# One decoder layer on one core: where the second half of the tokens gets the low parts of its weights

## The chip, the core and the metric

The kernel runs on one core of a Trainium2 chip. The metric is the device time of one launch, in microseconds (us). Three runs of the kernel before took 3326.43, 3331.45 and 3336.54 us; the median is 3331.45 us. One further run was recorded by the hardware profiler: it took 3347.84 us, of which 3346.1 us are the span of the recorded instructions. A matter of 0.3% (10 us) is about what a comparison of two versions can tell from no change.

The engines of the core are called PE (matrix products), DVE (vector work), ACT (activation functions and copies), POOL (here it issues the gathers) and SP (here it issues all other DMA transfers). Each engine works through its own instructions in a fixed order and waits on semaphores for the others.

## What is computed

One layer over 1024 tokens of width 1024, all in fp32:

```python
z = x @ w_in                       # 9 column groups, width 7184
ua = causal_depthwise_conv(lru_x)  # branch A: RG-LRU, 8 channel blocks, a scan over time
ya = rg_lru(ua) * gelu(lru_y)
yb = rmsnorm(gla_chunked(q, k, v, log_f)) * silu(gla_r)   # branch B: 4 heads
m = sigmoid(gate_a) * ya + sigmoid(gate_b) * yb
x = layer_norm(ALPHA * x + m @ w_out)
ple = sigmoid(x @ ple_gate_w) * (p @ ple_proj_w)
# PEER: 8 heads, 16 of 16384 one-neuron experts each
hid = gelu(einsum("td,ted->te", x, u_tab[idx]))
ffn = einsum("te,ted->td", gate * hid, v_tab[idx])
out = layer_norm(ALPHA * x + ffn + ple)
```

## The kernel before

The tokens are worked in two halves of 512 (`HT`). For each half, `mixer` projects the tokens, runs the two branches and merges them, and `post` does the output product, the first layer norm, the scores of the experts, and the gate of the per-layer input. Then come the experts. Four of the eight blocks of 128 tokens (`GT`) gather their experts' rows one by one: for each of 128 selections POOL gathers a u row for every token (`ug`, line 837), DVE multiplies and sums it (line 839), later POOL gathers v rows (`vg`, line 866) and PE adds them up, four gathers in eight products at a time (`ffn`, line 873). The gathered tiles take turns in seven buffers (`ROWS`), so a gather waits until DVE or PE is done with an older one. The other four blocks (`DT`) are worked in `dense`: all 16384 experts for 512 tokens, with a dense table of gates (`dense_gates`, line 978).

The gathers begin at the end of the first half and go on to the end of the program. A generator hands out their steps while the second half's mixer, its `post` and then `dense` are recorded; a scheduler then sets each engine's order by its own estimate of when things are ready. So changing one thing can shift every engine's order from there on.

An fp32 product is made of three products of a faster type: each operand is split into a high part (a rounded copy, made by ACT) and a low part (the rest, source minus high part, made by DVE), and `mm3` (lines 251 to 254) multiplies high by high, high by low and low by high. Weights come in pieces of 128 rows by 1024 columns of fp32 (512 KB). `weights` loads a piece (`raw`, line 261) and makes the high part `wh_...` and the low part `wl_...`, each with two buffers in turn. Both halves of the tokens use the same weights. In the first half the low part is split off by DVE (line 249) and, for the first `LOW` pieces, also written to DRAM (line 275); in the second half, where a stored low part exists, it is read back instead (line 266) and only ACT's copy (line 267) is made:

```python
        key = (src.tensor.name, src.offset)
        if low.get(key) is not None:
            nc.sync.dma_start(l.bitcast(F32), low[key])
            nc.scalar.activation(h, raw, AF.Copy)
        else:
            split(h, l, raw)
            if key not in low:
                n = len(low)
                low[key] = None
                if n < LOW:
                    low[key] = dram.tile(shape, F32, name=f"low{n}")
                    nc.sync.dma_start(low[key], l.bitcast(F32))
```

With `LOW = 60` these are the 56 pieces of a mixer (`zx`, `zy`, `ga`, `gr`, `gb`, `zv` eight each, `zq` and `zk` four each) and the first 4 of the 8 pieces of the output product (`mix`).

Of the kernel before, what the change touches and what calls it, by code (L numbers as in the profile page):

```python
# [50 lines left out]
ROWS = 7  # L51
RING = 10

LOW = 60

TG = 8

# [7 lines left out]
def kernel(ctx: ExitStack, tc: tile.TileContext, a: dict, out: bass.AP, tap=None):  # L65
# [190 lines left out]
    def weights(src, name, shape):  # L256
# [11 lines left out]
# [7 lines that stand above are left out]
# [898 lines left out]
```

## Time and profile before

| stretch of the span (us) | what runs | PE busy | DVE busy | PE clock | DMA share |
|---|---|---|---|---|---|
| 15 to 415 (400) | mixer, first half | 390.11 | 250.05 | 0.98 | 0.44 |
| 647 to 1120 (473) | mixer, second half, with gathers | 423.26 | 378.14 | 0.92 | 0.77 |
| 1120 to 1650 (530) | post, second half, gate table, gathers | 401.75 | 464.00 | 0.89 | 0.85 |
| 1650 to 3290 (1640) | dense experts, gathers | 1608.49 | 1010.23 | 0.99 | 0.92 |
| whole span 3346.1; profiled run 3347.84 | | 3034.9 | 2303.3 | 0.95 | |
| median of three runs 3331.45 | | | | | |

[...] DMA share is how busy the 16 DMA engines were. A stretch is read by asking which engine is nearly always busy in it, and, where none is, what the engines wait for.

### The profile page before, as it was taken

What the parts mean: (1) busy time and instruction counts of PE and PEld (TensorE: products, weight loads), DVE (VectorE), ACT (ScalarE), POOL (GpSimd) and SP (SyncE); (2) the same over time, 40 slices, a digit from 0 to 9 for tenths busy, and PEclk for the clock granted to TensorE, in tenths of its full rate; (3) what the DMA queues carried; (4) which work ended last, traced back from release to release, by engine and by line L of the source; (5) the groups of instructions that cost most, each with busy time, mean ns of one, the idle gap of its engine ahead of it and who ended that gap; (6) DMA issues with size and microseconds to landing.
All of it is one profiled execution on the core that took longest, in us unless ns stands there. A gap on an engine that the chain in (4) does not pass through costs nothing.

```text
span 3346.1 us, 48006 instructions
## 1 busy us (share of the span) xinstructions
PE 3034.9 (91%) x17160; PEld 2318.8 (69%) x17160; DVE 2303.3 (69%) x5663; ACT 1233.1 (37%) x2130; POOL 1175.8 (35%) x1034
## 2 busy tenths in 40 slices
PE   8999988797999879658599999999999999999995
PEld 6788777576777666448467777777777777776662
DVE  7556558987788899888887766666666666564333
ACT  6443323253244565558433332222232222232220
POOL 0000000533421445440344544454444444453442
PEclk9999989897999899889799999999999999999997
DMA  5444444787877899976889999999989999999886
GB/s 172 146 164 152 143 159 131 296 289 251 315 242 253 319 305 327 300 256 171 309 316 353 330 333 334 342 329 335 336 321 347 347 336 338 343 327 321 315 288 241
DMA packets 364302, 939.73 MB, mean 281 GB/s; under 512 B 33920, under 2 KB 115968, under 8 KB 359968
## 3 DMA queue, kind: packets, MB, share of 16 engines
q0 software_dynamic: 147456, 536.94, 44.9%
q1 hardware_dynamic: 216608, 399.74, 34.4%
q8 instruction: 134, 2.20, 0.3%
q14 instruction: 104, 0.85, 0.1%
HBM read 854.76 MB, written 81.79 MB: 280 GB/s over the span
## 4 chain that ended last, share of the span: by engine, by line
PE 70%; DVE 11%; DMA 9%; ACT 4%; issue 4%; POOL 1%; another core or an unknown queue 0%; SPq 0%; POOLq 0%; DVEq 0%; ACTq 0%
PE ph L252 7%; PE ph L253 7%; PE ph L254 7%; PE ffn L873 7%; PE pv L253 7%; PE pv L252 7%; PE pv L254 7%; DMA vg<-in_peer_v_dram,idxT 3%; DMA ug<-in_peer_u_dram,idx 3%; DVE ug L839 2%; PE pg L978 1%; PE pgr L252 1%; PE pgr L254 1%; PE pgr L253 1%; PE pri L340 1%
## 5 line engine op out<-in xcount | busy, mean ns | idle before, releaser
L837 POOL DMA_INDIRECT ug<-in_peer_u_dram,idx x512 | 594.3, 1161 | 1319.7 <-DVE bs L766 615.4
L866 POOL DMA_INDIRECT vg<-in_peer_v_dram,idxT x512 | 580.1, 1133 | 819.2 <-DVE ug L839 402.3
L839 DVE SCALAR_TENSOR_TENSOR ug<-ug,x1g 128x1024 f32<-128x1024 f32 x512 | 621.3, 1220 | 298.6 <-DMA ug<-in_peer_u_dram,idx 242.3
L252 PE MATMUL ph<-x1h,uh 128*128 128x512 f32 x1024 | 408.5, 399 | 13.7 <-ACT uh L248 13.7
L253 PE MATMUL ph<-x1l,uh 128*128 128x512 f32 x1024 | 407.4, 398 | 0.0
L254 PE MATMUL ph<-x1h,ul 128*128 128x512 f32 x1024 | 406.4, 397 | 0.0
L253 PE MATMUL pv<-vl,wdh 128*128 128x512 f32 x1024 | 404.3, 395 | 0.3 <-DVE vl L249 0.3
L254 PE MATMUL pv<-vh,wdl 128*128 128x512 f32 x1024 | 400.4, 391 | 0.0
L252 PE MATMUL pv<-vh,wdh 128*128 128x512 f32 x1024 | 375.4, 393 | 24.0 <-ACT wdh L248 24.0
L248 ACT ACTIVATE vh<-vr 128x512 fp32r<-128x512 f32 x256 | 160.9, 631 | 567.8 <-PE pv L254 284.4
L873 PE MATMUL ffn<-vg,w 128*32 128x512 f32 x2048 | 264.5, 637 | 81.3 <-DMA vg<-in_peer_v_dram,idxT 80.4
L249 DVE TENSOR_TENSOR vl<-vr,vh 128x512 fp32r<-128x512 f32 x256 | 174.9, 688 | 207.0 <-ACT vh L248 177.6
L248 ACT ACTIVATE uh<-ur 128x512 fp32r<-128x512 f32 x256 | 160.3, 628 | 328.7 <-PE ph L253 233.2
L252 PEld LDWEIGHTS pv<-vh,wdh 128*128 128x128 f32 x1024 | 192.5, 188 | 76.7 <-ACT wdh L248 25.7
L252 PEld LDWEIGHTS ph<-x1h,uh 128*128 128x128 f32 x1024 | 192.4, 188 | 76.7 <-ACT uh L248 16.5
L249 DVE TENSOR_TENSOR ul<-ur,uh 128x512 fp32r<-128x512 f32 x256 | 175.1, 686 | 95.0 <-ACT uh L248 70.6
L253 PEld LDWEIGHTS pv<-vl,wdh 128*128 128x128 f32 x1024 | 192.8, 188 | 66.8 <-issue 16.8
L253 PEld LDWEIGHTS ph<-x1l,uh 128*128 128x128 f32 x1024 | 192.6, 188 | 57.3 <-issue 13.4
L254 PEld LDWEIGHTS ph<-x1h,ul 128*128 128x128 f32 x1024 | 192.4, 188 | 55.6 <-issue 8.4
L254 PEld LDWEIGHTS pv<-vh,wdl 128*128 128x128 f32 x1024 | 192.1, 188 | 46.5 <-issue 6.7
L873 PEld LDWEIGHTS ffn<-vg,w 128*32 128x32 f32 x2048 | 55.5, 113 | 215.9 <-issue 121.8
L978 PE MATMUL pg<-oi,oj 128*128 128x128 f32 x1024 | 165.4, 302 | 33.1 <-ACT oi L977 16.7
(475 smaller groups left out, 6056.2 us busy)
## 6 DMA issues: line engine op xcount, KB each, us to landing
ur<-in_uT_dram SPq DMA_DIRECT2D x256, 256.0 KB
vr<-in_peer_v_dram SPq DMA_DIRECT2D x256, 256.0 KB
g_d<-gst SPq DMA_DIRECT2D x32, 1024.0 KB
gt<-g_d SPq DMA_DIRECT2D x32, 1024.0 KB
raw_zx<-in_w_z_dram SPq DMA_DIRECT2D x16, 512.0 KB
raw_zv<-in_w_v_dram SPq DMA_DIRECT2D x16, 512.0 KB
raw_zy<-in_w_z_dram SPq DMA_DIRECT2D x16, 512.0 KB
raw_ga<-in_w_z_dram SPq DMA_DIRECT2D x16, 512.0 KB
```

What stands on the lines that cost most here:

```text
L248: nc.scalar.activation(h, src, AF.Copy)
L249: nc.vector.tensor_tensor(l, src, h, op=ALU.subtract)
L252: nc.tensor.matmul(o, wh, xh, start=first, stop=False)
L253: nc.tensor.matmul(o, wh, xl, start=False, stop=False)
L254: nc.tensor.matmul(o, wl, xh, start=False, stop=last)
L340: nc.tensor.matmul(o, wri[:, i, j], ua[:, i], start=True, stop=True)
L837: nc.gpsimd.indirect_dma_start(out=ug, out_offset=None, in_=a["peer_u"], in_offset=bass.IndirectOffsetOnAxis(ap=idx[:, s:s + 1], axis=0))
L839: nc.vector.scalar_tensor_tensor(ug, ug, 1.0, x1, op0=ALU.mult, op1=ALU.mult, accum_out=hid[:, s:s + 1])
L866: nc.gpsimd.indirect_dma_start(out=vg, out_offset=None, in_=a["peer_v"], in_offset=bass.IndirectOffsetOnAxis(ap=idxT[:, t:t + 1], axis=0))
L873: mm = nc.tensor.matmul(ffn[32 * c:32 * c + 32, e * 512:(e + 1) * 512], w32[:, c, r], rows_v[c][:, e * 512:(e + 1) * 512], start=ph == 0 a ...
L978: nc.tensor.matmul(o[:, r], oj[:, t], oi, start=True, stop=True)
```

## The change

```diff
-LOW = 60
+LOW = 0
```

With `LOW = 0` no low part is stored, so none is read back: the 60 stores of line 275 in the first half and the 60 read-backs of line 266 in the second are gone (31.5 MB each way), and the second half splits its 60 pieces itself: ACT's copy is made at line 248 instead of 267, the same copy, and DVE makes 60 more subtractions (line 249). A `raw` buffer, which ACT's copy alone used to free, is now freed by DVE's subtraction. Since the scheduler works from the new program, the second half is ordered anew on PE, DVE, ACT and SP. POOL's order is the same. At three places:

On DVE, in the second half's mixer at the end of the second head (`oT` and `m` are the head's output, `v`, `i` and `sc` belong to the routing of tokens to experts, `ug` to the gathers). Before:

```order
L474 SCALAR_TENSOR_TENSOR oT<-oT,gla_norm_g,pb 128x512 x2
L452 SCALAR_TENSOR_TENSOR tr<-tr,pgr 128x512
L480 TENSOR_TENSOR oT<-oT,tr 128x512
L839 SCALAR_TENSOR_TENSOR ug,hid<-ug,x1g 128x1024 x2
L484 SCALAR_TENSOR_TENSOR oT<-tb,oT 128x512
L485 TENSOR_TENSOR m<-m,oT 128x512
L725 MAX v_8057<-sc 128x8
L726 MAX_INDEX i_8058<-v_8057,sc 128x8
L727 MATCH_REPLACE sc<-v_8057,sc 128x128
L728 MAX v_8057<-sc 128x8
```

Now:

```order
L474 SCALAR_TENSOR_TENSOR oT<-oT,gla_norm_g,pb 128x512 x2
L249 TENSOR_TENSOR wl_gr<-raw_gr,wh_gr 128x1024
L725 MAX v_7937<-sc 128x8
L452 SCALAR_TENSOR_TENSOR tr<-tr,pgr 128x512
L726 MAX_INDEX i_7938<-v_7937,sc 128x8
L480 TENSOR_TENSOR oT<-oT,tr 128x512
L727 MATCH_REPLACE sc<-v_7937,sc 128x128
L728 MAX v_7937<-sc 128x8
L729 MAX_INDEX i_7938<-v_7937,sc 128x8
L839 SCALAR_TENSOR_TENSOR ug,hid<-ug,x1g 128x1024
L725 MAX v_7937<-sc 128x8
L249 TENSOR_TENSOR wl_gb<-raw_gb,wh_gb 128x1024
```

What moved: the low parts of the next weights (`gr`, `gb`) stand in DVE's row between the work of the head, the routing and the gathers.

On SP, in the same mixer, at the loads for the third head. Before:

```order
L266 DMA wl_gb<-low_2172 128x1024
L261 DMA raw_zk<-in_w_z_dram 128x1024
L266 DMA wl_zq<-low_2209 128x1024
L261 DMA raw_zv<-in_w_v_dram 128x1024
L266 DMA wl_zk<-low_2244 128x1024
L261 DMA raw_zv<-in_w_v_dram 128x1024
L743 DMA sc<-sc_d 128x512
L266 DMA wl_zv<-low_2314 128x1024
```

Now:

```order
L261 DMA raw_gb<-in_w_z_dram 128x1024
L261 DMA raw_zq<-in_w_z_dram 128x1024
L261 DMA raw_zk<-in_w_z_dram 128x1024
L261 DMA raw_zv<-in_w_v_dram 128x1024
L743 DMA sc<-sc_d 128x512
L261 DMA raw_zv<-in_w_v_dram 128x1024
```

What moved: the read-backs, each of which stood between two loads of `raw`, are gone, and the loads follow each other.

On PE, the end of the program (`pv` is the last dense product, `ffn` the gathered rows; eight products of 32x512 are four gathers). Before:

```order
L253 MATMUL pv_28811<-vl,wdh 128x512
L254 MATMUL pv_28811<-vh,wdl 128x512
L252 MATMUL pv_28811<-vh,wdh 128x512
L253 MATMUL pv_28811<-vl,wdh 128x512
L254 MATMUL pv_28811<-vh,wdl 128x512
L873 MATMUL ffn<-vg,w_25491 32x512 x32
```

Now:

```order
L254 MATMUL pv_28691<-vh,wdl 128x512
L252 MATMUL pv_28691<-vh,wdh 128x512
L253 MATMUL pv_28691<-vl,wdh 128x512
L254 MATMUL pv_28691<-vh,wdl 128x512
L873 MATMUL ffn<-vg,w_25371 32x512 x16
```

What moved: sixteen gathers (x32) stood behind the last dense product, now eight (x16); the other eight stand among the dense products. Up to the first dense product 160 products of `ffn` stood before and 168 now, of 1024.

## Rows read from the trace of the kernel before

**Rows 1.** The page's first line and its engine row for PE and DVE.

```profile
span 3346.1 us, 48006 instructions
...
PE 3034.9 (91%) x17160; PEld 2318.8 (69%) x17160; DVE 2303.3 (69%) x5663; ACT 1233.1 (37%) x2130; POOL 1175.8 (35%) x1034
```

**Rows 2.** Busy time by stretch (from:to, length, engines, PE clock, DMA share, GB/s).

```profile
core 0: us, PE busy (x) PEld busy (x) DVE busy (x) ACT busy (x) POOL busy (x), PEclk, DMA share, GB/s
15.00:415.00 400.00, 390.11 (x2710) 314.38 (x2710) 250.05 (x590) 177.86 (x240) 0.00 (x0) 0.98 0.44 151
647.00:1120.00 473.00, 423.26 (x2770) 332.81 (x2769) 378.14 (x1046) 184.75 (x246) 156.42 (x126) 0.92 0.77 273
1120.00:1650.00 530.00, 401.75 (x2696) 326.75 (x2694) 464.00 (x1297) 334.56 (x759) 206.00 (x162) 0.89 0.85 283
1650.00:3290.00 1640.00, 1608.49 (x7680) 1170.76 (x7680) 1010.23 (x2038) 466.49 (x776) 767.62 (x698) 0.99 0.92 331
```

**Rows 3.** The same columns for the second half's mixer in five pieces.

```profile
650.00:750.00 100.00, 91.78 (x525) 68.27 (x526) 86.29 (x182) 57.63 (x69) 41.05 (x31) 0.95 0.85 311
750.00:850.00 100.00, 79.14 (x556) 63.29 (x556) 71.44 (x169) 29.13 (x42) 37.70 (x30) 0.83 0.73 264
850.00:950.00 100.00, 95.68 (x606) 77.21 (x605) 80.11 (x212) 38.48 (x53) 33.17 (x27) 0.97 0.79 289
950.00:1050.00 100.00, 94.33 (x654) 76.82 (x652) 88.93 (x308) 39.49 (x54) 24.16 (x21) 0.95 0.72 248
1050.00:1120.00 70.00, 60.06 (x428) 45.72 (x426) 48.37 (x175) 17.02 (x28) 17.96 (x17) 0.88 0.71 242
```

**Rows 4.** Groups by line: a split in 0:600, the gathers' product in 647:1120.

```profile
L249 DVE TENSOR_TENSOR wl_gb<-raw_gb,wh_gb 128x1024 fp32r<-128x1024 f32 x8 | 9.8, 1225 | 18.3 <-ACT wh_gb L248 18.3
...
L839 DVE SCALAR_TENSOR_TENSOR ug<-ug,x1g 128x1024 f32<-128x1024 f32 x117 | 139.8, 1217 | 18.7 <-DMA ug<-in_peer_u_dram,idx 17.1 <-DMA x1g<-x_d 1.6
```

**Rows 5.** Waits of PE, then of DVE, in 647:1120 (total us, times, longest).

```profile
PE po L550 <- DVE AT L545: 20.2, 6, 6.7
PE pzv L253 <- DMA wl_zv<-low: 1.5, 2, 1.2
PE pzy L254 <- DMA wl_zy<-low: 1.3, 2, 0.9
...
DVE ug L839 <- DMA ug<-in_peer_u_dram,idx: 17.1, 6, 4.7
```

**Rows 6.** SP's longest wait in 647:1120 (total us, times, longest).

```profile
SPq L266 <- PE pgr L254: 87.8, 7, 33.7
```

**Rows 7.** The chain of work in 647:1120, the read-backs on it (start, us).

```profile
783.81 6.96 DMA wl_gr<-low
...
940.69 3.48 DMA wl_zy<-low
```

**Rows 8.** PE's timeline at 886 us, a wait in brackets.

```profile
886.10 3.58 PE L461 MATMUL pn<-ones,sq 128*128 128x1 f32 x16 [2.76 <-ACT sq L457]
```

**Rows 9.** Busy time behind that wait, columns as in the stretches above.

```profile
886.00:893.00 7.00, 6.90 (x25) 6.20 (x26) 5.45 (x22) 0.05 (x1) 2.26 (x2) 0.53 0.98 392
893.00:903.00 10.00, 10.00 (x49) 8.21 (x48) 6.91 (x12) 1.54 (x2) 3.70 (x3) 1.00 0.55 194
```

**Rows 10.** Group of PE by line in 1650:3290, the gathered rows.

```profile
L873 PE MATMUL ffn<-vg,w 128*32 128x512 f32 x1632 | 198.7, 605 | 10.6 <-DMA vg<-in_peer_v_dram,idxT 10.6
```

**Rows 11.** PE's timeline at the end of the program.

```profile
3291.29 0.40 PE L254 MATMUL pv<-vh,wdl 128*128 128x512 f32 x1
3294.72 2.82 PE L873 MATMUL ffn<-vg,w 128*32 128x512 f32 x16 [3.04 <-DMA vg<-in_peer_v_dram,idxT]
3302.20 3.64 PE L873 MATMUL ffn<-vg,w 128*32 128x512 f32 x16 [4.66 <-DMA vg<-in_peer_v_dram,idxT]
3310.45 3.64 PE L873 MATMUL ffn<-vg,w 128*32 128x512 f32 x16 [4.61 <-DMA vg<-in_peer_v_dram,idxT]
3323.13 3.48 PE L873 MATMUL ffn<-vg,w 128*32 128x512 f32 x16 [9.05 <-DMA vg<-in_peer_v_dram,idxT]
```

## Prediction, made before the changed kernel was run

> **What bounds the kernel now.** The profiled execution has a span of 3346.1 us, of which PE is busy 91% and DVE 69% [rows 1]; the time of that execution is 3347.84 us. An average like this hides where the change acts, so I read the busy time by stretch next [rows 2]. In the first half's mixer PE is busy 390.11 of 400 us and DVE 250.05, with the splits in it: PE bounds it. In the second half's mixer PE is busy 423.26 of 473 us and DVE 378.14: neither is full, each waits for the other in turn. In 1120:1650, the work behind the mixer, DVE (464.00 of 530) is the busier one. In the dense stretch PE is (1608.49 of 1640). The change adds DVE work to the second of these four stretches, so I cut that into pieces [rows 3]: DVE is busy 86.29, 71.44, 80.11 and 88.93 per 100 us, and 48.37 in the last 70. The room under 100 is therefore uneven, and it is smallest in 650:750 and 950:1050. The waits name what PE stands for there: first of all the attention matrix AT that DVE makes (20.2 us, 6 times), and hardly the read-backs (1.5 and 1.3 us) [rows 5]. The chain of waits, which follows single releases, does run through four read-backs [rows 7]. Last comes the end of the program, where PE has no dense products left and waits for gathered rows [rows 11].
>
> **The change, part by part.**
>
> First half: the 60 stores go. No engine reads what they write before the second half, and PE is busy 97% of the stretch without them mattering [rows 2]. The DMA share there is 0.44, so the loads beside them were not held up much. I take 0; PE's idle 9.9 us bounds what could be won, and nothing is added, so the bounds are -3 (a third of it) and 0.
>
> Second half, splits: 60 subtractions of a 128x1024 piece. The same instruction takes 1225 ns in the first half; beside gathers DVE's product of the same size and with two inputs takes 1217 ns [rows 4]. I take 1.22 us. Four of the 60 are in the output product, 56 in the mixer: 56 x 1.22 = 68.3 us in 473 us, or 14.4 per 100 and 10.1 per 70. ACT's copies stay as they are. DVE is in order, and a split waits for the raw piece, for ACT's copy, and for PE to leave the older of two wl buffers. Behind a waiting split stand the head's decay and AT steps, the routing, and the gathers' products (the order rows of DVE above show them mixed), and behind those PE (for AT and for wl) and POOL (for free gather buffers). A full DVE therefore reaches PE.
>
> How much of 68.3 us finds cover? The fullest piece in which PE was still nearly full had DVE at 88.93 per 100 with PE at 94.33 [rows 3]. I take this share as what DVE can be filled to before PE is lengthened one for one. The room is then 88.93 less what is busy: 2.6, 17.5, 8.8 and 0, and in the last piece 62.3 - 48.4 = 13.9. Uncovered are 14.4 - 2.6 = 11.8, 0, 14.4 - 8.8 = 5.6, 14.4, and 0: together +31.8 us, rounded to +32. The bounds: DVE can be filled to 100, which leaves 0.7 + 3.3 = +4; nothing finds cover, because the splits come when DVE is needed for something else, +68. I choose between them by the nearest row there is, since no row of this stretch shows DVE above 89.
>
> Read-backs: 60 DMAs of 512 KB go, from SP's queue too. There each waited for PE to leave a wl buffer (87.8 us for wl of gr alone, in 7 waits [rows 6]), with the next raw loads and the routing's loads of sc queued behind it; now those go out earlier, but a raw buffer is freed one step later, by DVE. What PE itself lost to read-backs was 1.5 + 1.3 us and less [rows 5]: -3. The chain gives them more, from 6.96 to 3.48 us for the first and last of four, some 24 us in all [rows 7], but a part of that ran beside other PE work. So -3, bounded by 0 and -24. Less traffic may shorten DVE's wait for u rows too (17.1 us [rows 5]), but that is room on DVE and not time on PE, and it lies inside the bounds of the splits.
>
> Moved gathers: up to the end of the mixer five more u products are in DVE's row now (+6.1 us at 1217 ns), and four splits of the output product come behind (+4.9); in return nine products fewer stand between the end of `post` and the first dense work (46 against 55, -11.0). I take 0 for this in 1120:1650, bounds -6 and +6.
>
> Dense: one more group of four gathers stands among the dense products (168 products against 160 before them, and eight gathers fewer behind: so eight gathers moved, four of them to ahead of dense). A gather group of sixteen records takes 16 x 198.7 / 1632 = 1.95 us [rows 10]: +2.
>
> The tail: behind the last dense product stood four groups of four gathers, now two. Their starts are 7.48 and 8.25 us apart for the first two, then 12.68 [rows 11]: POOL's gathers set this pace, not PE. With two groups fewer the first two steps go: -15.7, so -16. This needs the gathers to be that much earlier, which a later start of dense gives them: POOL's order is the same and its gathers run on while the mixer lasts longer. If they are not, it is 0.
>
> The sum on the profiled execution: 0 + 32 - 3 + 0 + 2 - 16 = +15, so 3363. That execution is 16.4 us above the median of the runs, so on the median it is 3331.45 + 15 = 3346 us, 0.4% slower.
>
> **The rivals.** *Faster: DVE's idle time swallows the splits.* For it speaks that DVE idles 95 us of 473 in the mixer [rows 2], that the same splits in the first half cost PE nothing, and that a split has the time of a whole weight piece on PE. Against it: the routing, the gathers and AT want DVE there at the same time. DVE is filled to 100: 4 - 3 + 2 - 16 = -13, so 3318; with the chain's 24 us for the read-backs, 4 - 24 + 2 - 16 = -34, so 3297. It wins by more than 10 us where DVE can be filled to about 98 (8 us uncovered), or where the read-backs are worth much more than 3.
>
> *Same: DVE can be filled to 95.* Uncovered are then 5.7 + 0 + 0 + 8.3 + 0 = 14: 14 - 3 + 2 - 16 = -3, so 3328.
>
> *Slower by more: the clock.* [...] Over the whole stretch: PE idles 49.7 us in 473 where the first half has 9.9 in 400, and is busy 33.2 us longer, at 0.92 against 0.98 [rows 2]; 33.2 / 39.8 = 0.83 us for each us of idle. The uncovered 32 us, if they are waits of PE and not work that merely spreads, then cost 32 x 0.83 = 27 more: +42, so 3373. Against it: a part of this lower clock is already in the stretch and does not get worse.
>
> [...]
>
> *Slower by much: no cover at all.* Each split stands in front of something that PE is waiting for: 68 - 3 + 2 - 16 = +51, so 3382. This is the mechanism of one in-order DVE with a wl wait at its head. Against it: PE is the fuller engine in 850:950 (95.68 to 80.11 [rows 3]).
>
> *The tail stays.* With the uncovered 32 and no shorter tail, 32 - 3 + 2 = +31, so 3362; it lies inside the range. That the change does not do what it says is ruled out: none of the read-back and store rows is left in the new program's order.
>
> **How the numbers follow.** About 0.3% (10 us) is what can be told from no change. Chances: the forecast (3346, its own range 3341 to 3360, the long tail with it) 0.34, same 0.29, faster 0.21, the clock 0.10, no cover 0.06. So slower 0.50, same 0.29, faster 0.21. The range reaches from 3315, which takes in the nearer half of the faster case, to 3378, which leaves out no cover: some 0.15 lies outside.
>
> **What would show it.** DVE's share in the second mixer: about 89 in every piece confirms the step on cover, 95 and more means the rivals that are not slower. The start of the first dense product moves later by about the uncovered time (some 30 us) if the sum is right. PE's waits should name wl from DVE, and AT from DVE for more than 20.2 us, in place of wl from DMA. PE's clock in 647:1120 below 0.92 points to the clock. Two groups behind the last dense product, with the end some 36 us behind the first of them, confirm the tail. I am wrong if the first dense product starts no later, or if the second half's mixer gets shorter with fuller engines.

## The result, and the profile after

The changed kernel is slower: 3370.14 us (median of 4, 3359.19 to 3376.31) against 3330.79 us, a ratio of 1.0105 with a 95% interval of 1.0084 to 1.0127. In a later comparison the two took 3364.80 and 3320.26 us, 1.0124 (1.0103 to 1.0144). The forecast was 3346, 0.4% slower; the change costs 1.0 to 1.2%. The direction was right and the time lies in the range, but the size was missed by more than a factor of two. (A ratio here is the one on record for all runs of its comparison; the quotient of the two medians can differ from it by some 0.1%.)

The page of the profiled execution (3366.56 us), its first line and its engine row, to set beside [rows 1]:

```profile
span 3364.8 us, 47867 instructions
...
PE 3047.6 (91%) x17160; PEld 2325.0 (69%) x17160; DVE 2370.6 (70%) x5723; ACT 1235.7 (37%) x2132; POOL 1182.2 (35%) x1034
```

DVE has 60 instructions more and is busy 67.3 us longer. Busy time by stretch, columns as in [rows 2] (PEclk is the clock that PE was granted, as a share of its full clock):

```profile
15.00:415.00 400.00, 390.52 (x2707) 314.49 (x2708) 250.19 (x588) 176.34 (x238) 0.00 (x0) 0.98 0.23 78
647.00:1120.00 473.00, 395.07 (x2484) 311.65 (x2488) 410.35 (x988) 177.84 (x234) 156.81 (x116) 0.89 0.58 198
```

The first half is what it was (PE busy 390.52; the DMA share fell from 0.44 to 0.23). The second stretch is not: PE is busy 395.07 of 473 us where it was 423.26. The same mixer in five pieces, as in [rows 3]:

```profile
650.00:750.00 100.00, 80.65 (x450) 58.76 (x451) 93.69 (x164) 49.96 (x59) 43.93 (x33) 0.86 0.70 248
750.00:850.00 100.00, 84.45 (x504) 68.61 (x503) 81.60 (x166) 35.73 (x49) 39.21 (x29) 0.91 0.62 212
850.00:950.00 100.00, 84.96 (x548) 66.62 (x547) 80.32 (x213) 25.35 (x38) 29.31 (x25) 0.86 0.56 191
950.00:1050.00 100.00, 79.31 (x585) 65.32 (x584) 87.90 (x285) 30.63 (x43) 24.15 (x17) 0.86 0.45 148
1050.00:1120.00 70.00, 63.74 (x398) 51.75 (x400) 63.83 (x160) 33.17 (x44) 17.71 (x12) 0.95 0.55 185
```

In the first piece DVE goes over the 88.93 that the forecast let it reach, and PE has 80.65 where it had 91.78. In the last DVE goes over it too (63.83 of 70), while PE has 63.74 where it had 60.06. In 750:1050 between them DVE stays at 80 to 88, and PE has 79 to 85, where the last 200 us of that had 94 to 96 before. The mixer ends later now, so a piece does not hold the same work as it did. The new waits of PE, then those of DVE, in 647:1120 (total us, times, longest), to set beside [rows 5]:

```profile
PE pA L526 <- DVE qs L506: 25.3, 3, 10.6
PE po L550 <- DVE AT L545: 19.2, 5, 6.8
PE pri L340 <- DVE ua L330: 9.8, 2, 9.6
```

```profile
DVE oT L474 <- PE pb L471: 18.2, 3, 6.6
DVE ms L464 <- PE pn L461: 9.4, 2, 5.0
...
DVE ug L839 <- DMA ug<-in_peer_u_dram,idx: 3.0, 4, 1.8
```

PE waits for `qs`, a step of the head's decay on DVE, 25.3 us in three waits; in the first trace of before it waited a tenth of that:

```profile
PE pA L526 <- DVE qs L506: 2.5, 2, 1.6
```

The wait for AT is as long as it was (19.2 against 20.2), and wl from DVE is no long wait (0.8 and 0.6 us). DVE's wait for u rows is gone but for 3.0 us (17.1 before). DVE meanwhile waits for PE more than it did, 18.2 us for `pb` alone (3.8 before): the two engines wait for each other in turn. SP's longest wait is no longer one for PE, as in [rows 6], but for DVE, which now frees `raw`:

```profile
SPq L261 <- DVE wl_zy L249: 56.1, 7, 14.8
```

The end of the program, as in [rows 11]: behind the last dense product stand two groups of gathers, not four, and the span ends 40 us behind it where it ended 55 us behind.

```profile
3325.13 0.40 PE L254 MATMUL pv<-vh,wdl 128*128 128x512 f32 x1
3328.88 3.33 PE L873 MATMUL ffn<-vg,w 128*32 128x512 f32 x16 [3.35 <-DMA vg<-in_peer_v_dram,idxT]
3341.97 3.61 PE L873 MATMUL ffn<-vg,w 128*32 128x512 f32 x16 [9.76 <-DMA vg<-in_peer_v_dram,idxT]
```

### The profile page after: what moved, and what is told of

It reads as the page before. It is cut to its first block, busy times and chain, and to the rows that moved or that the text cites. A ratio compares the mean times of both kernels' runs of the same rounds, so it can differ in the third digit from the quotient of the medians.

```text
span 3364.8 us, 47867 instructions
## 1 busy us (share of the span) xinstructions
PE 3047.6 (91%) x17160; PEld 2325.0 (69%) x17160; DVE 2370.6 (70%) x5723; ACT 1235.7 (37%) x2132; POOL 1182.2 (35%) x1034
## 4 chain that ended last, share of the span: by engine, by line
PE 68%; DVE 12%; DMA 9%; issue 4%; ACT 4%; POOL 2%; another core or an unknown queue 0%; SPq 0%; POOLq 0%; DVEq 0%; ACTq 0%
PE ffn L873 7%; PE ph L254 7%; PE ph L253 7%; PE ph L252 6%; PE pv L253 6%; PE pv L254 6%; PE pv L252 6%; DVE ug L839 3%; DMA vg<-in_peer_v_dram,idxT 3%; DMA ug<-in_peer_u_dram,idx 2%; PE pg L978 2%; POOL ug L837 1%; PE pgr L252 1%; DMA vr<-in_peer_v_dram 1%; PE pgr L253 1%
## 5 line engine op out<-in xcount | busy, mean ns | idle before, releaser
L837 POOL DMA_INDIRECT ug<-in_peer_u_dram,idx x512 | 609.4, 1190 | 1317.2 <-DVE bs L766 613.4
L866 POOL DMA_INDIRECT vg<-in_peer_v_dram,idxT x512 | 571.5, 1116 | 833.5 <-DVE ug L839 392.9
```

Of the source, the lines that this page charges most:

```text
L837: nc.gpsimd.indirect_dma_start(out=ug, out_offset=None, in_=a["peer_u"], in_offset=bass.IndirectOffsetOnAxis(ap=idx[:, s:s + 1], axis=0))
L866: nc.gpsimd.indirect_dma_start(out=vg, out_offset=None, in_=a["peer_v"], in_offset=bass.IndirectOffsetOnAxis(ap=idxT[:, t:t + 1], axis=0))
```

## The experiments

In the ratios below each kernel is set against runs of the kernel before that were made together with it on the same chip. The medians of the kernel before differed from one such set to the next (3320 to 3338 us), so times are compared within a set only. The edits are shown in part. Three theories stood at the start: the loss is DVE's added work (1), or the loss of the read-backs and the new order of the program (2), or the read-backs were worth much by themselves (3).

### What was removed, what was added

**Neither read-back nor split.**

```diff
+        if kept and shape[1] in fixed:
+            l = fixed[shape[1]]
+            nc.scalar.activation(h, raw, AF.Copy)
+            return h, l
```

> Left out: the second half neither reads a low part back nor splits it; every piece of a shape uses the low part of the first piece of that shape (two splits in all), and no low part is stored. Theory 1 (DVE's added work makes the second mixer's decay steps late, so PE waits; the read-backs were worth next to nothing): as fast as the kernel before or a little faster, 3318 to 3333 us, with the second mixer's last product of gb at about 1120 to 1135 us as before (1126.5) and no wait of PE for qs above 3 us. Theory 2 (the read-backs gone and the new order cost the time, whatever DVE does): slow as the changed kernel, 3360 us and more. Theory 3 (the read-backs cost much, as the chain said): 3305 us or less.

1.0048 (1.0033 to 1.0064): none of the three. There is no added work, the last product of `gb` stands at 1113 in its trace, no later than before, and yet the program is slower. (The traced run took 3327.36 us, 9 us less than this kernel's median, so its trace need not show where the time goes.) The held orders below explain it.

**Read-back and split both**, the split into the raw tile:

```diff
             nc.scalar.activation(h, raw, AF.Copy)
+            nc.vector.tensor_tensor(raw, raw, h, op=ALU.subtract)
```

> The low part is stored and read back as before, and DVE makes the subtraction too, into the raw tile where nobody reads it. Theory 1 (DVE's work): slow as the changed kernel or a little slower, 3365 to 3385 us, the second mixer longer by some 45 us. Theory 2 (read-backs gone and order): as before, 3331 us. Theory 3 (read-backs cost much): 3385 us and more.

1.0153 (1.0126 to 1.0180): as theory 1 expects.

**The stores kept**, and the second half split:

```diff
         if low.get(key) is not None:
-            nc.sync.dma_start(l.bitcast(F32), low[key])
-            nc.scalar.activation(h, raw, AF.Copy)
+            split(h, l, raw)
```

> The changed kernel with the 60 stores of the first half kept; nothing reads them. All theories that put the loss into the second half: the same as the changed kernel, 3360 to 3376 us, with the first mixer's stretch 15:415 unchanged (PE busy 390). If the stores did cost the first half something that the change gave back: slower than the changed kernel by that, 3380 us and more.

1.0126 (1.0100 to 1.0152): the same as the changed kernel. The stores cost the first half nothing.

**Every other piece.**

```diff
-                if n < LOW:
+                if n < LOW and n % 2 == 0:
```

> Every other one of the 60 pieces is stored and read back, the other 30 are split in the second half. Theory 1 with a cost in proportion to DVE's work: half of the loss, 3345 to 3355 us. If DVE's free time could take up the first half of the work: 3328 to 3338 us. If one late step costs as much as many: 3360 us and more.

1.0155 (1.0124 to 1.0186): half the work costs as much as all of it. Together with the first kernel this says that something besides the work counts. Each of these kernels has its own order, since the scheduler works anew from each program, so an experiment on the work was one on the order too.

### Where PE waits: the decay steps on DVE

A head is worked in two units. For each, DVE makes a chain of some 28 short instructions, from the first `qk` to `qP`; PE can begin with `pA` when the last `qs`, near its end, is done. PE's timeline in the changed kernel (its second trace), first head, second unit:

```profile
763.32 0.39 PE L254 MATMUL pzx<-xh,wl_zx 128*128 128x512 f32 x1
774.31 0.47 PE L526 MATMUL pA<-qs,ks 128*64 128x64 f32 x2 [10.60 <-DVE qs L506]
```

PE's products of `zx`, which cover the chain, end at 763.7; `pA` begins 10.60 us later. DVE's timeline in that gap:

```profile
763.96 0.28 DVE L514 TENSOR_TENSOR al<-al 128x128 f32<-128x128 f32 x1
764.16 0.28 DVE L508 TENSOR_TENSOR qk<-k__6141,Qd 128x128 f32<-128x128 f32 x1
764.61 1.22 DVE L249 TENSOR_TENSOR wl_gb<-raw_gb,wh_gb 128x1024 fp32r<-128x1024 f32 x1 [0.16 <-ACT wh_gb L248]
765.75 0.74 DVE L330 SCALAR_TENSOR_TENSOR ua<-zx,conv_w,ua 128x512 f32<-128x512 f32 x1
766.41 1.22 DVE L839 SCALAR_TENSOR_TENSOR ug<-ug,x1g 128x1024 f32<-128x1024 f32 x1
...
768.71 0.28 DVE L506 TENSOR_TENSOR qk<-q__6102,al 128x128 f32<-128x128 f32 x1
768.91 0.28 DVE L513 TENSOR_TENSOR Qd<-Qd,al 128x128 f32<-128x128 f32 x1
769.11 1.40 DVE L330 SCALAR_TENSOR_TENSOR ua<-zx,conv_w,ua 128x512 f32<-128x512 f32 x2
770.44 0.28 DVE L514 TENSOR_TENSOR al<-al 128x128 f32<-128x128 f32 x1
...
773.97 0.28 DVE L506 TENSOR_TENSOR qs<-q__6102,al 128x128 f32<-128x128 f32 x1
```

A step of the chain is 0.28 us. Between one group of steps and the next (764.16, 768.71, 770.44) DVE does a split, convolutions (`ua`) and products of the gathers of 0.7 to 1.2 us each. DVE is hardly idle here, while PE waits for the chain's last short steps. I added up the time from the first `qk` to `qP` in DVE's timeline over the eight units: 144 us in the kernel before, 207 in the changed kernel, 215 with every other piece split, 145 with neither. By an estimate from 28 steps of 0.28 us a chain alone takes 8 us, and in the changed kernel the splits are 4 to 10 us of a drawn-out one; the rest is gathers' products, routing and convolutions that the new order put there.

### Work and order apart

To tell the two apart I held a program to another's order: edges from each instruction to the next, along the list of the other, for PE, DVE and ACT, with the added splits left free. Where it is the changed kernel's order, SP's loads are held too, and the pin that queues the gathers' steps behind DVE's latest instruction is left out.

```diff
+            own = [i for i in nc.cur_bb.bb.instructions
+                   if i.engine == e and not type(i).__name__.startswith("BassTile") and i.name not in extra]
...
+                if last is not None:
+                    tc.add_manual_dep(own[n], last.name, mybir.DependencyInfo(
+                        mybir.DependencyClass.NoSync, mybir.DependencyReason.DATA), reason="order")
+                last = own[n]
```

**The changed kernel's work in the order of before:**

> The changed kernel's work (60 splits more, no stores, no read-backs) in the order of the kernel before: PE, DVE and ACT are held to the order that they had before, instruction by instruction, and only the 60 splits are put in between on DVE. Theory 1 (work: DVE's 60 subtractions cost the time wherever they stand): as slow as the changed kernel, 1.0 to 1.5% over the kernel before, the second mixer longer by some 45 us. Theory 2 (order: the new order draws out DVE's decay steps, 205 us in all eight against 144; the subtractions themselves find cover): within 0.4% of the kernel before, eight decay stretches of 150 to 165 us in all, and no wait of PE for qs above 4 us.

**The work of before in the changed kernel's order:**

> The work of the kernel before (stores and read-backs, no split in the second half) in the changed kernel's order: PE, DVE, ACT and the loads on SP are held to the changed kernel's order, with the 60 splits left out of it. Theory 1 (work): as the kernel before, within 0.4%. Theory 2 (order): slower by 0.6 to 1.4%, with waits of PE for qs of 5 to 10 us as in the changed kernel, if somewhat shorter since the splits are missing in them.

**No read-backs and no splits, in the order of before:**

> Left out: the second half neither reads a low part back nor splits it, but for the first piece of each of two shapes, whose low part all others use; nothing is stored. PE, DVE and ACT are held to the order of the kernel before. Whatever differs from the kernel before is what the stores and read-backs cost by themselves. Theories 1 and 2: 0 to 10 us faster, 0.997 to 1.000 (PE lost 3 us to read-backs). If the chain's 24 us were right: 0.993. The same kernel without the held order took 1.0048: if that was the order, it is gone here; if it is gone through something else, it stays.

And later, **no read-backs and no splits in the changed kernel's order:**

> Left out: the second half neither reads a low part back nor splits it (but for the first piece of each of two shapes, whose low part the others use). PE, DVE, ACT and the loads on SP are held to the changed kernel's order. With read-backs this order took 1.0059. If the order itself costs that, and the read-backs next to nothing (0.2% in the order of before): 1.003 to 1.006. If the read-backs are what is slow in this order: 0.997 to 1.001.

| | order of before | order of the changed kernel |
|---|---|---|
| neither read-back nor split | 0.9980 (0.9962 to 0.9998) | 1.0080 (1.0064 to 1.0096) |
| read-backs | 1 | 1.0059 (1.0041 to 1.0077) |
| splits | 1.0113 (1.0087 to 1.0138) | 1.0105 and 1.0124 |

Theory 2 expected the splits to be free in the first column, and they aren't: with them the old order is as slow as the new one. Theory 1 expected nothing of the new order in the first two rows, and it costs 0.6% with the read-backs and 1.0% without (1.0080 against 0.9980), with no work added. 1.0080 lies above both ranges that were set for it (1.003 to 1.006 and 0.997 to 1.001). In the old order the 60 splits cost 1.3% against nothing at all; in the new one 0.25 to 0.45%. So the two costs don't add up: the splits alone are enough for the loss, the new order alone costs half of it or more, and together they cost no more than the splits in the old order. How the loss of the changed kernel is to be shared out between the two, these runs do not settle; they show that the work makes it slower in either order and that the new order gains nothing. The read-backs are worth 0.2% in the old order; in the new one the kernel without them is not faster. The first kernel's 1.0048 was its order: held, the same program takes 0.9980.

How the work costs in the old order: the busy times of the second mixer without and with the splits, from 647 to some 5 us behind the start of its last product (traces of one set of runs), and PE's waits with them:

```profile
647.00:1120.00 473.00, 429.08 (x2811) 337.79 (x2812) 390.13 (x1068) 189.34 (x256) 156.63 (x129) 0.92 0.65 219
```

```profile
647.00:1164.00 517.00, 438.14 (x2807) 342.17 (x2805) 450.07 (x1122) 188.60 (x255) 163.60 (x129) 0.89 0.60 199
```

```profile
PE po L562 <- DVE AT L557: 18.6, 5, 6.2
PE pzy L263 <- DVE wl_zy L258: 15.5, 3, 8.7
PE pA L538 <- DVE qs L518: 8.3, 4, 3.2
```

DVE is busy 59.9 us more and the mixer 44 us longer. The eight chains take 158 us here, as theory 2 expected of this kernel, but the time isn't back: the loss does not need a drawn-out chain. PE's idle time rises from 43.9 to 78.9 us, and its busy time by 9 us at a clock of 0.89 instead of 0.92. Of the idle time 15.5 us are waits for a split of `zy` itself; the rest is spread over waits for other steps on DVE (`qs` 8.3 against 3.7, and AT, `qP`, S and `Qd` 2 to 3 us more each). Behind the mixer's last product the two traces differ by 7 us in all. In the new order PE waits for the decay steps instead, also with no split there (the kernel with the work of before, its chains 203 us):

```profile
PE pA L539 <- DVE qs L519: 19.9, 4, 7.3
PE po L563 <- DVE AT L558: 16.8, 6, 6.1
```

**How the cost grows with the work**, in the order of before, with 30 and 120 subtractions:

> Every other of the 60 pieces is split in the second half, the other 30 are read back; PE, DVE and ACT are held to the order of the kernel before. In proportion (each subtraction costs some 0.7 us wherever it stands): half of what 60 cost, 1.004 to 1.007. Bent (DVE's free time covers the first ones, and only a full DVE costs): 0.998 to 1.002. Not by number at all, as the same work in its own order looked: 1.010 and more.

> All 60 pieces are split in the second half, and each subtraction is made twice (the second one into the raw tile, which nobody reads any more), in the order of the kernel before. 120 subtractions are 137 us in a second mixer where DVE idled 84 us. In proportion: 1.024 to 1.030. Bent upwards, since DVE is full now: 1.03 and more, the second mixer longer by over 110 us.

```profile
647.00:1133.00 486.00, 428.35 (x2802) 338.40 (x2801) 415.28 (x1090) 185.73 (x253) 155.31 (x128) 0.92 0.70 242
```

```profile
647.00:1204.00 557.00, 449.69 (x2818) 349.72 (x2817) 510.19 (x1174) 189.15 (x255) 167.52 (x128) 0.86 0.56 184
```

Subtractions 0, 30, 60, 120: 0.9980, 1.0027 (1.0015 to 1.0038), 1.0113, 1.0252 (1.0231 to 1.0273). Against 0 that is 0.5%, 1.3% and 2.7%, or 16, 44 and 90 us at 3324 us, where the subtractions are 37, 73 and 146 us at 1.22 (of the 16 us some 3 are the 30 read-backs that are left). So 0.35 to 0.6 of the work has no cover, from the first 30 on, though DVE idled 83 of 473 us with none. The first 30 are the cheapest: 1.0027 lies between the range for a cost in proportion (1.004 to 1.007) and that for free ones (0.998 to 1.002). The 1.0155 of the half that was left to its own order is order for the most part.

### The gathers' anchors

```diff
-        return next(i for i in reversed(nc.cur_bb.bb.instructions) if i.engine == e)
+        return next(i for i in reversed(nc.cur_bb.bb.instructions) if i.engine == e and i.name not in splits)
```

> The changed kernel, but the gathers' steps are queued behind the last DVE instruction that is not one of the 60 splits (as in the kernel before; in the changed kernel many of them are queued behind a split, which DVE does early). If these anchors are what let the products into the decay steps: at least half of the loss comes back, ratio 1.000 to 1.006. If not, the scheduler draws them out by itself: 1.009 to 1.015. Its order has 10 or 11 products of the gathers in two of the eight decay stretches, as the changed kernel has 10 and 18, so the second is likelier.

1.0124 (1.0096 to 1.0152): with the anchors of before the time is not back; the eight chains take 217 us in this kernel, whose order is again its own.

### Both kernels again, and two other ways

> The kernel before once more, for a second trace of it and for what two runs of one kernel differ by. The first profiled execution took 3347.84 us, 9 to 26 us over the medians seen so far; the changed kernel's took 3366.56, 4 under its median. If that execution was a slow one of its kind: a span of 3320 to 3340 us here, ratio 0.998 to 1.002, and then the changed kernel's trace is 25 to 45 us longer than this one, where it was 18.7 us longer than the first. If profiled executions of this kernel are always that much over the others: 3340 us and more.

> The changed kernel once more, on the same chip as the others of this call. 1.009 to 1.014; its second mixer ends within 3 us of where it did (last product of gb at 1174), since two traces of nearly the same program (with the stores and without) agreed to 1 us there. The end of the program, behind the last dense product: 38 to 42 us, against 55 in the kernel before.

0.9999 (0.9985 to 1.0014) and 1.0124. The second trace of the kernel before has a span of 3322.6 us, that of the changed kernel 3367.7. The first traces (3346.1 and 3364.8) understated the difference, 18.7 us against 45.1; the medians of this set differ by 44.5. First and last product of the mixer's `gb`, of the dense `ph`, which opens that part, and of the dense `pv`, which closes it (line, duration min/median/max in ns, first to last start), kernel before, then changed:

```profile
L254 PE MATMUL pgb<-xh,wl_gb x128: 393/396/505, 115.3 to 1113.5; 128*128 128x512 f32 x128
...
L252 PE MATMUL ph<-x1h,uh x1024: 388/396/793, 1588.9 to 3207.6; 128*128 128x512 f32 x171
...
L254 PE MATMUL pv<-vh,wdl x1024: 387/389/504, 1664.5 to 3267.4; 128*128 128x512 f32 x171
```

```profile
L254 PE MATMUL pgb<-xh,wl_gb x128: 392/396/632, 115.0 to 1174.4; 128*128 128x512 f32 x128
...
L252 PE MATMUL ph<-x1h,uh x1024: 389/396/503, 1610.9 to 3269.6; 128*128 128x512 f32 x171
...
L254 PE MATMUL pv<-vh,wdl x1024: 387/389/628, 1704.1 to 3328.6; 128*128 128x512 f32 x171
```

**POOL instead of DVE:**

```diff
-            nc.sync.dma_start(l.bitcast(F32), low[key])
             nc.scalar.activation(h, raw, AF.Copy)
+            nc.gpsimd.tensor_tensor(l, raw, h, op=ALU.subtract)
```

> The 60 subtractions of the second half made by POOL instead of DVE; no stores, no read-backs. POOL is busy 156 of 473 us in the second mixer. Theory 1 (DVE's added work is what costs): 0.996 to 1.005, with the second mixer ending at 1110 to 1135. If POOL's in-order queue makes the gathers late behind a split that waits for a buffer, or POOL takes several us for a subtraction so that PE waits for it: 1.01 and more, with waits of PE for wl from POOL and of DVE for u rows well over 20 us.

1.0233 (1.0207 to 1.0259): the worst of the versions with 60 splits; its rows stand in the last section.

**Four more pieces:**

```diff
-LOW = 60
+LOW = 64
```

> All 64 pieces are stored and read back, four more than before (the rest of the output product). DVE has four subtractions less (4.9 us) in a stretch where it is busy 464 of 530 us. Theory 1: 0.997 to 1.001. If a new order by itself is worth as much as was seen for the kernel with neither splits nor read-backs (1.0048 in its own order, 0.998 in the order of before): up to 1.005 in either direction.

0.9970 (0.9954 to 0.9986): a little faster than both kernels. It has four splits less and an order of its own; which of the two gains, no run here shows.

## Why the prediction was wrong

The forecast's terms beside the two traces of one set of runs (the second traces, [rows 1 to 11] being those of the first):

| step | forecast, us | measured, us |
|---|---|---|
| first half, stores gone | 0 | 0 |
| second mixer: splits +32, read-backs -3 | +29 | +60.9 (last `gb` 1113.5 to 1174.4) |
| from there to the first dense product `ph`: moved gathers | 0 | -38.9 (475.4 to 436.5) |
| from there to the last `pv`: dense | +2 | +39.2 (1678.5 to 1717.7) |
| tail | -16 | -16.1 (55.2 to 39.1) |
| sum | +15 | +45.1 |

**First half: right.** PE busy 390.10 and 390.06 in the second traces, and the kernel with the stores kept is no slower than the one without.

**Splits: the term that was mis-sized.** The step that failed is "I take this share as what DVE can be filled to before PE is lengthened one for one". The forecast read this off rows of the old order, so the kernel held to that order tests it: 44 us of the mixer's 68 found no cover, where 32 were taken. 34.9 of the 44 are idle time of PE, near the 32; the other 9.1 are busy time at a lower clock (0.89 against 0.92), so it was not one for one. The same rule gives 12 and 93 us for 30 and 120 subtractions, where the last product of `gb` moved by 13 and 83 (1127.6 and 1198.3 against 1114.8), so the size of the share is not far off in the old order. In the new one it was no limit of that kind: in 750:1050 DVE stayed at 80 to 88 and PE fell to 79 to 85. DVE's idle time had been counted as room, piece by piece, but DVE idles where it waits for PE (in the first trace of the changed kernel 18.2 us for `pb` and 9.4 for `pn`) or for gathered rows (3.0), and at other times is full while PE waits for one short step out of it (10.60 us for `qs` in the second).

**A part of the miss is the clock.** The mixer in the second traces, kernel before, then changed:

```profile
647.00:1119.00 472.00, 426.98 (x2813) 336.80 (x2813) 387.53 (x1067) 187.63 (x254) 157.09 (x131) 0.93 0.79 284
```

```profile
647.00:1180.00 533.00, 446.26 (x2824) 346.23 (x2824) 452.96 (x1137) 190.86 (x256) 178.97 (x137) 0.88 0.60 201
```

PE's idle time rises from 45.0 to 86.7 us, +41.7, and its busy time by 19.3 at a clock of 0.88 instead of 0.93, for the same products: 427 x 0.93 and 446 x 0.88 are 397 and 393. The forecast had +29 of idle and no busy time; the rival "slower by more: the clock" had 32 and 27 and came out at 3373. Its price was too high, 0.83 for each us of idle against 19.3 / 41.7 = 0.46 (of its 33.2 us some 7 were more work and no clock: 423.26 x 0.92 and 390.11 x 0.98 are 389 and 382), and its idle time too low, and the two nearly made up for each other. The price is no constant: in the old order the splits brought 9.1 us of busy time with 34.9 of idle, 0.26. The rival got 0.10; the trace of before spoke for more, since in it a wait of PE of 2.76 us [rows 8] was followed by 7 us at a mean clock of 0.53 [rows 9]. In the first six of them, 886 to 892, it was 0.50, and products of `pgr` start 0.43 us apart there; from 893 on it was 1.00, and they start 0.23 us apart. The mixer with more idle time of PE had the lower clock too (0.88 with 86.7 us, 0.93 with 45.0). That a wait by itself brings the clock down, the runs do not show.

**Read-backs: about right.** -3 was taken; 0.2% (0.0 to 0.4) is 7 us of the whole program, and the mixer with none of them and the same order ends at 1114 as with them in the second trace. The chain's 24 us were not theirs to give back.

**A new wait: half right.** The waiting split was named, with the head's steps behind it. In the old order PE does wait for wl (15.5 us for `zy`). In the changed kernel the scheduler gives the splits their place ahead of PE's need, and the wait moves to `qs` (25.3 us), which was not named.

**The new order: its cost was not in the sum.** Two moved groups of gathers were taken as -16, and they came. In all the sum had 0 + 2 - 16 = -14 for what the new order does, and nothing for what it does to the mixer. By the ratios the changed kernel is as slow as the same work in the old order (1.0105 and 1.0124 against 1.0113): the new order is worth -3 to +4 us, not -14, and the work 38 us where +29 was taken, each of these give or take some 10 us. The trace of the new order with read-backs and no split shows where the gain went: its last `gb` stands at 1165.9, 52 us later than in the second trace of before, the way from there to the first dense product is 36 us shorter, the dense part 27 us longer, the tail 17 us shorter.

**Behind the mixer: right by luck.** 0 and +2 were forecast, with bounds of 6 us for the first; -38.9 and +39.2 came, and they cancel. Some 76 products of the gate table (`pg`) that stood ahead of the first dense product now stand behind it, and PE idles 22 us less ahead of it and 20 us more behind it. A later start of that product was to confirm the sum, and a start no later to refute it. In the first pair of traces, before and then changed, it starts no later:

```profile
L252 PE MATMUL ph<-x1h,uh x1024: 389/396/792, 1609.5 to 3231.3; 128*128 128x512 f32 x171
```

```profile
L252 PE MATMUL ph<-x1h,uh x1024: 389/396/628, 1609.7 to 3265.8; 128*128 128x512 f32 x171
```

In the second it starts 22 us later (1588.9 to 1610.9), where some 30 were named. This product was no good mark for the mixer's length, since the new order moved it against the work ahead of it.

**The base.** 3347.84 was set 16.4 us over the median and the difference carried over. The difference of one pair of traces can be off by more than that: 18.7 and 45.1 us in two pairs. In the first pair the table's terms behind the first half are +47.4, -47.2, +33.6 and -15.1.

**Rivals.** "DVE's idle time swallows the splits" and "the same" fall: DVE was at 85% (452.96 of 533) in the changed mixer, and PE waited more. (At 98 the first gives 8 - 3 + 2 - 16 = -9, a little less than the 10 us that were written.) "No cover at all" had +51, near the +45.1, but not by its mechanism: in the old order a third of the work is covered, and what fills the 61 us up in the new one came with the order, which gives it back behind the mixer.

## What to carry to other kernels

An engine's idle time beside a busier one is only in part room for more work when the two hand small steps to and fro: ask which step the other engine is waiting for, and how far added work stretches the chain that ends in it; here 0.35 to 0.6 us was lost for each us of added vector work, on an engine that had been busy 82% of the stretch. Where a scheduler orders the program, an edit is always two edits; hold the order before saying what the work costs, since the same program took 0.998 or 1.005 by its order alone. Compare more than one pair of traces before a difference of half a per cent is explained.

## What the runs showed of the hardware

POOL took twice as long as DVE for the same subtraction, 2.4 to 3.1 us against 1.22, and DVE's own instructions grew longer beside it. POOL's splits, then three of DVE's groups in that kernel and the same three in the kernel before, and the busy times of that mixer:

```profile
L267 POOL TENSOR_TENSOR wl_zy<-raw_zy,wh_zy 128x1024 fp32r<-128x1024 f32 x8 | 24.7, 3107 | 38.4 <-ACT wh_zy L266 38.4
...
L267 POOL TENSOR_TENSOR wl_zx<-raw_zx,wh_zx 128x1024 fp32r<-128x1024 f32 x8 | 19.2, 2396 | 5.3 <-ACT wh_zx L266 5.2
```

```profile
L838 DVE SCALAR_TENSOR_TENSOR ug<-ug,x1g 128x1024 f32<-128x1024 f32 x118 | 174.4, 1500 | 8.6 <-DMA ug<-in_peer_u_dram,idx 8.2 <-DMA x1g<-x_d 0.4
L513 DVE TENSOR_TENSOR al<-al 128x128 f32<-128x128 f32 x56 | 30.6, 546 | 0.9
...
L359 DVE TENSOR_TENSOR_SCAN iu<-c,h_last,iu 128x512 f32<-128x512 f32 x8 | 18.1, 2308 | 0.0
```

```profile
L839 DVE SCALAR_TENSOR_TENSOR ug<-ug,x1g 128x1024 f32<-128x1024 f32 x120 | 143.5, 1218 | 21.4 <-DMA ug<-in_peer_u_dram,idx 19.5 <-DMA x1g<-x_d 1.9
...
L514 DVE TENSOR_TENSOR al<-al 128x128 f32<-128x128 f32 x56 | 16.0, 286 | 1.0
...
L360 DVE TENSOR_TENSOR_SCAN iu<-c,h_last,iu 128x512 f32<-128x512 f32 x8 | 9.8, 1265 | 0.0
```

```profile
647.00:1203.00 556.00, 454.11 (x2801) 354.89 (x2801) 495.19 (x1056) 187.18 (x252) 298.51 (x184) 0.86 0.56 182
```

The gathers' product takes 1500 ns instead of 1218, the scan 2308 instead of 1265, the product of two parts of `al` 546 instead of 286. DVE is busy 495.19 us with none of the splits to do, against 387.53: giving 56 subtractions to POOL cost DVE 108 us, more than making them itself would (56 x 1.22 = 68). Sorted by whether one of POOL's splits ran beside them, the records of that trace show where the time went (POOL's spans are rough): 93 of the gathers' products ran beside none and took 1217 ns, 25 ran beside one and took 2555; of the products of `al` 49 took 286 and 7 took 2362; all eight scans ran beside one. Three of the `MAX8` of line 727, which read one tile, ran beside one and took 291 ns, against 286 for the others. The group of `Qd` products kept its 285 ns; only one of its 48 ran beside a split. Why some instructions took longer beside a split and others did not, these records do not show.

The products of split operands were faster than direct fp32 products, even at three for one. In the first trace of before, three fp32 products of 128x512 (`pri`, line 340, two records of 592 ns each) take 2.74 us from 46.28 on, and nine products of `pzq` of that size, which stand for three, take 2.26 us from 36.68 on, both at a clock of 1.00.
